# A hybrid S5 and attention decoder block: opening by single row tiles, modulation matmuls between product blocks, heads innermost in the bias table, gate row through DRAM

## Chip, cores and metric

The kernel runs on one core of a Trainium2 chip. The metric is the device time of one execution in microseconds, as the median of several runs. All times in the profile are microseconds from the start of the profiled execution's span.

## What is computed

One decoder block for 256 positions of width 2048, in float32. A conditioning vector c gives six modulation vectors (shift, scale and gate, for two sub-layers); the first sub-layer has an S5 and an attention branch side by side, the second is an MLP.

```
mod = silu(c) @ w_ada + b_ada                      # 2048 x 12288
sh1, sc1, g1, sh2, sc2, g2 = split(mod, 6)
h = rms_norm(x, g_mix) * (1 + sc1) + sh1
u, q, k, v, ga, gb = split(h @ w_in, ...)          # 2048 x 8192
y_ssm = s5_branch(u, ...)                          # complex scan, GELU, GLU
y_att = attention(q, k, v, rel_bias)               # 8 heads of 128, causal, T5 bias by distance
merged = sigmoid(ga) * (y_ssm @ w_proj_ssm) + sigmoid(gb) * (y_att @ w_proj_attn)
x = x + g1 * (merged @ w_out)
h2 = rms_norm(x, g_mlp) * (1 + sc2) + sh2
x = x + g2 * (square(relu(h2 @ w_ff1)) @ w_ff2)
out = rms_norm(x, g_final)
```

All 256 positions lie in one attention block, so attention is plain causal attention with a bias that depends on head and distance.

## The kernel before

**Products.** Every weight is read once from DRAM, in tiles of 128 rows by 1024 columns (512 KB). `stream` loads a tile into `wraw` (L132, L134; seven buffers), ScalarE casts it to a rounded high part `whi` and VectorE subtracts to get the low part `wlo` (`split`, L139 and L141; four buffers each). A product of activations and weights is then three matmuls: high by high, high by low and low by high (L171 to L173 in `gemm_t`, L209 to L211 in `gemm_n`, L185 and L187 in `gemm_d`). A tile of w_in costs 24 such matmuls in `gemm_t`, in eight column blocks `blk` of 128.

**Row tiles.** The 2048 columns of h are 16 row tiles `kt` of 128. h is kept transposed, as high and low part `ah` and `al`. Tile `kt` of h needs the matching 128 entries of scale and shift, `A1` and `B1`, and these need 128 columns of w_ada each.

**Order.** The instructions are written in program order, and a scheduler orders each engine's list at build time from priorities (`high_priority`) and explicit orders (`after`: not before that instruction on the same engine). At the end of each streamed tile `step` takes jobs out of *lanes*, each with its rate in jobs per tile. The lane `ada` carries the w_ada work, `ssm` the S5 tables, `second` what completes the opening, `xr` the scaling of x by the norm.

**Opening.** x (transposed) is loaded, `norm1` sums its squares with TensorE against a matrix of ones and makes the row R of reciprocal norms. For the first four row tiles, w_ada is multiplied on TensorE in `ada_first`: c stands as one column in a matrix of zeros (`cz`), four 32-column matmuls side by side (L240), a copy of the sums (L244), and a fold by a column of ones (L247). This is done in two halves of two row tiles, for scale and shift each, with 256 columns and four loads of 512 KB apiece. The first half precedes all products; the second (`second`) follows the second product tile. Then `scale1` (L369) multiplies x by R, and `make_h1` (L376 and `split`) makes h.

**The rest of w_ada.** For the other 12 row tiles `ada_job` loads rows of the transposed w_ada into the shared `wraw` buffers (L261), and VectorE multiplies with `cb`, the broadcast of silu(c), and sums along the row (L268): four loads of 512 KB for two row tiles' scale, four for their shift. `cb` comes by a one-partition row `crow`, a DRAM tile `cd`, and a broadcast load of 1 MB (L883). The lane runs at 1.65 jobs a tile until the ninth row tile's h is there, then at 0.8. The same kind of job later gives the two gates and the second modulation.

**Products of w_in.** The product units are walked as (columns, first and last row group), with row groups of 4, 6 and 6 row tiles: first q, k, v and u for row tiles 0 to 3, then the gate columns for 0 to 9 (its result is copied by L932), then four units over 4 to 9, and so on.

**Bias table.** `bias_prep` makes the bias by distance as 8 rows (one for each head) of 383, and one DMA on GpSimd's queue writes it 32 times into DRAM (`scr`, L397). `bias_load` reads it back skewed, so that partition p holds the bias of query p: `tz`, with head outermost (L404). `attn1` adds `tz` to the scores (L655, L656).

**Gate rows.** `ada_bcast` turns four columns of a modulation vector into a row on all partitions: four matmuls of a broadcast column against the identity (L288) and a copy by ScalarE (L290). It serves g1 and g2; g2's row `g2b` is first read when the MLP's next to last block of the second product ends.

Of the kernel before, what the change touches and what calls it, by code (L numbers as in the profile page):

```python
# [75 lines left out]
class Kern:  # L76
# [35 lines left out]

    def lane(self, name, jobs, rate, credit=0.0):
        self.lanes[name] = [list(jobs), rate, credit]
# [44 lines left out]
    def gemm_t(self, src, kts, c0, xh, xl, koff=0, mid=None):  # L159
# [3 lines left out]
        for i, (kt, hi, lo) in enumerate(self.stream(src, kts, c0)):  # L163
# [3 lines left out]
            for blk in range(8):  # L167
# [5 lines left out]
                self.mm = nc.tensor.matmul(o, lo[:, c], xh[:, kx, :], start=False, stop=sp, skip_group_check=True)  # L173
        return banks
# [42 lines left out]
    def ada_first(self, j, half, done, home=None):  # L217
        nc = self.nc
        n = 2 * (1 - j) + half
        st = {}  # L220

        def load(i):
            if home is None:
                w = st[i] = self.wp.tile([P, 1024], F32, name="wraw", tag="wraw", bufs=7)
            else:
                w = st[i] = home[:, i, :]
            with self.after(self.last):
                ld = nc.sync.dma_start(w, self.a["wan"][j, half, i])
            if self.early or home is not None:
                self.last = ld  # L230

        def total(i):
            w = st.pop(i).rearrange("p (k n) -> p k n", k=4)
            if i == 0:
                st["p"] = self.aux("adap")
            p = st["p"][:, 0:256]
            with self.after(None if self.early else self.mm):
                for k in range(4):
                    q = 32 * k
                    nc.tensor.matmul(p[q:q + 32, :], self.cz[:, 4 * i + k, :], w[:, k, :], start=i == 0,  # L240
                                     stop=i == 3, tile_position=(0, q), skip_group_check=True)
            if i == 3:
                acc = self.s4[:, 512 + 256 * n:768 + 256 * n]
                nc.scalar.copy(acc, p)  # L244
                pc = self.tmp("adac")
                for k in range(2):
                    self.adac = nc.tensor.matmul(pc[:, k:k + 1], acc[:, k * P:(k + 1) * P], self.ones[:, 0:1],  # L247
                                                 start=True, stop=True)
                done(pc[:, 0:2])
        return [(lambda i=i: load(i), lambda i=i: total(i)) for i in range(4)]  # L250

    def ada_job(self, vec, k0, n, done):
# [4 lines left out]
        def load(i):  # L257
            w = st[i] = self.wp.tile([P, 1024], F32, name="wraw", tag="wraw", bufs=7)
# [17 lines left out]
    def ahead(self, units):  # L276
# [5 lines left out]
        return [lambda i=i: job(i) for i in range(len(units) + 1)]  # L282

# [82 lines left out]
    def scale1(self, k0, gate=None):  # L366
        x = self.x[:, k0:k0 + 2, :]
        with self.after(gate):
            self.nc.vector.tensor_mul(x, x, self.R[:, None, :].to_broadcast([P, 2, S]))  # L369

    def make_h1(self, k0, A, B, fine=False):
        nc = self.nc
        h = self.big.tile([P, 2, S], F32, name="htmp", tag="htmp", bufs=1)
        for k, kt in enumerate((k0, k0 + 1)):
            with self.after(self.done[-1][1] if fine and k else None):
                nc.scalar.activation(h[:, k, :], self.x[:, kt, :], AF.Identity, scale=A[:, kt:kt + 1],  # L376
                                     bias=B[:, kt:kt + 1])
            if fine:
                self.split(self.ah[:, kt, :], self.al[:, kt, :], h[:, k, :])
        if not fine:  # L380
            self.split(self.ah[:, k0:k0 + 2, :], self.al[:, k0:k0 + 2, :], h)

    def bias_prep(self):
        nc, a = self.nc, self.a
        self.tt = self.slot("T", [P, 2, 1024], name="tt")
        oh, vec = self.tt[0:32, 0, 0:VL], self.tt[0:H, 1, 0:VL]
        rb = self.cp.tile([32, H], F32, name="rb", tag="rb")
        nc.gpsimd.dma_start(oh, a["onehot"])
        nc.gpsimd.dma_start(rb, a["rel_bias"])
        p = self.aux("bv")  # L390
        with self.after(self.mm):
            nc.tensor.matmul(p[0:H, 0:VL], rb, oh, start=True, stop=True)
        with self.after(self.done[-1][0]):
            nc.vector.tensor_copy(vec[:, 0:256], p[0:H, 0:256])
        nc.vector.memset(vec[:, 256:VL], NEG)
        self.scr = self.dr.tile([H, 32, VL], F32, name="scr")
        nc.gpsimd.dma_start(self.scr, vec[:, None, :].to_broadcast([H, 32, VL]))  # L397

    def bias_load(self):
        self.tz = self.slot("T", [P, H, S], name="tz")  # L400
        s = self.scr
        for g in range(4):
            src = bass.AP(tensor=s.tensor, offset=s.offset + 127 - 32 * g, ap=[[VL - 1, 32], [32 * VL, H], [1, S]])
            self.nc.gpsimd.dma_start(self.tz[32 * g:32 * g + 32], src)  # L404
# [106 lines left out]
    def ssm_cc(self):  # L511
        self.cc = self.slot("QT", [P, 2, 32, 4, 16], name="cc")
# [30 lines left out]
    def ssm_build1(self, part):  # L543
        c = self.cmp
        if part == 0:
            self.bp = self.slot("VT", [P, 2, 32, 4, 16], name="bp")
        bp = self.bp
# [68 lines left out]
    def ssm_builds(self):  # L616
        return ([self.bias_prep, self.ssm_load_bc] + [lambda: None] * 2 + [self.ssm_cc]
                + sum([self.parts(self.ssm_build1, i) for i in range(4)], [])
# [28 lines left out]
    def attn1(self, h):  # L647
# [7 lines left out]
        v.scalar_tensor_tensor(s[:, 0:128], p[:, 0:128], scale, self.tz[:, h, 128:256], op0=OP.mult, op1=OP.add)  # L655
        v.scalar_tensor_tensor(s[:, 128:384], p[:, 128:384], scale, self.tz[:, h, :], op0=OP.mult, op1=OP.add)  # L656
# [144 lines left out]
    def body(self):  # L801
        nc, a, v = self.nc, self.a, self.nc.vector
        with self.hot():
# [3 lines left out]
            crow = self.slot("S3", [P, D], name="crow")[0:1]  # L807
            nc.sync.dma_start(crow, a["c"])
# [472 lines left out]
```

## Time and profile before

| | us |
|---|---|
| median of 3 runs | 1431.3 (1429.15 to 1432.28) |
| profiled execution | 1430.27 |
| its span | 1428.5 |
| TensorE busy, whole span | 1376.4 |
| VectorE busy | 1055.6 |
| ScalarE busy | 706.0 |
| first product matmul starts | 27.39 |

The program moves 354.51 MB by DMA, a mean of 248 GB/s; nearly all are weight tiles on SP's queue. The busy time of TensorE counts matmuls from start to modelled end, so it holds waits shorter than a matmul's length. "PE" in the rows is TensorE, "PEld" its weight loads, "DVE" VectorE, "ACT" ScalarE, "POOL" GpSimd, "SP" the engine that issues most loads; "SPq" and "POOLq" are their DMA issues. In a timeline row the first two numbers are start and length, and the brackets at its end give the idle time before it and what ended that.

### The profile page before, as it was taken

The numbers are of one execution on the slowest core, as the hardware profiler recorded it, in microseconds if no ns is written. First come the engines' busy times: TensorE is split into PE (matmuls) and PEld (weight loads), VectorE is DVE, ScalarE is ACT, GpSimd is POOL, SyncE is SP. The second block draws the span as 40 slices with busy tenths as digits, with TensorE's granted clock in tenths as the row PEclk, the third lists the DMA queues.
The fourth block names the chain that finished last, engine by engine and source line by source line (L and its number), as shares of the span: only waits on it lengthen the run. The fifth ranks groups of instructions, "written<-read, shape, count | busy, mean of one in ns | idle before, by whom it ended". The sixth has DMA issues, their size and how long they took to land.

```text
span 1428.5 us, 23983 instructions
## 1 busy us (share of the span) xinstructions
PE 1376.4 (96%) x9562; PEld 1238.9 (87%) x9562; DVE 1055.6 (74%) x1509; ACT 706.0 (49%) x916; POOL 39.4 (3%) x90
## 2 busy tenths in 40 slices
PE   5889999999999999999899999999999999999996
PEld 4789999989989999988799988888888888888885
DVE  5887999876798788977686685778666555555676
ACT  4554444346645743445554555535363553635444
POOL 1000000400002100000000000000000000000000
PEclk9999999999999999999999999999999999999998
DMA  9999885786447998887598568778767566566551
GB/s 368 383 352 337 309 287 165 236 270 228 145 153 234 322 339 299 303 319 276 182 353 285 171 233 281 228 260 287 254 224 263 170 200 192 177 206 187 182 205 60
DMA packets 111491, 354.51 MB, mean 248 GB/s; under 512 B 12137, under 2 KB 12169, under 8 KB 111121
## 3 DMA queue, kind: packets, MB, share of 16 engines
q1 hardware_dynamic: 108482, 348.19, 71.3%
q0 software_dynamic: 2896, 4.79, 1.3%
q8 instruction: 75, 1.23, 0.3%
q14 instruction: 38, 0.31, 0.1%
HBM read 348.33 MB, written 2.50 MB: 246 GB/s over the span
## 4 chain that ended last, share of the span: by engine, by line
PE 82%; DVE 8%; DMA 6%; ACT 2%; issue 2%; DVEq 0%; SPq 0%; ACTq 0%
PE pd L185 12%; PE pn L209 11%; PE pn L210 11%; PE pn L211 11%; PE pt L171 9%; PE pt L173 9%; PE pt L172 9%; PE pd L187 6%; DMA wraw<-in_w_in_dram 4%; DVE wlo L141 2%; DVE wraw L268 2%; ACT whi L139 1%; DMA ahm<-in_wan_dram 1%; DMA wraw<-in_w_proj_attn_dram 1%; PE trv L564 1%
## 5 line engine op out<-in xcount | busy, mean ns | idle before, releaser
L139 ACT CAST whi<-wraw 128x1024 fp32r<-128x1024 f32 x456 | 476.1, 1052 | 597.7 <-PE pn L210 160.1
L141 DVE TENSOR_TENSOR wlo<-wraw,whi 128x1024 fp32r<-128x1024 f32 x456 | 553.6, 1223 | 278.4 <-ACT whi L139 276.3
L185 PE MATMUL pd<-h2h,whi 128*128 128x512 f32 x768 | 266.8, 395 | 0.4 <-DVE part L1156 0.4
L171 PE MATMUL pt<-ah,whi 128*128 128x256 f32 x896 | 251.4, 288 | 12.0 <-ACT ah L139 6.8
L172 PE MATMUL pt<-ah,whi 128*128 128x256 f32 x896 | 251.2, 286 | 0.0
L173 PE MATMUL pt<-ah,wlo 128*128 128x256 f32 x896 | 241.6, 288 | 5.2 <-DVE wlo L141 4.7
L268 DVE SCALAR_TENSOR_TENSOR wraw<-wraw,cb 128x1024 f32<-128x1024 f32 x176 | 213.9, 1220 | 0.0
L187 PE MATMUL pd<-h2h,wlo 128*128 128x256 f32 x768 | 209.0, 280 | 0.0
L210 PE MATMUL pn<-whi,ff 128*128 128x512 f32 x512 | 199.2, 389 | 0.0
L209 PE MATMUL pn<-whi,ff 128*128 128x512 f32 x512 | 198.5, 390 | 0.0
L171 PEld LDWEIGHTS pt<-ah,whi 128*128 128x128 f32 x896 | 172.2, 194 | 15.8 <-ACT ah L139 7.0
L211 PE MATMUL pn<-wlo,ff 128*128 128x512 f32 x512 | 182.9, 389 | 0.0
L173 PEld LDWEIGHTS pt<-ah,wlo 128*128 128x128 f32 x896 | 166.8, 194 | 8.5 <-DVE wlo L141 8.2
L172 PEld LDWEIGHTS pt<-ah,whi 128*128 128x128 f32 x896 | 173.5, 194 | 0.2
L185 PEld LDWEIGHTS pd<-h2h,whi 128*128 128x128 f32 x768 | 142.5, 188 | 32.0 <-issue 0.7
L187 PEld LDWEIGHTS pd<-h2h,wlo 128*128 128x128 f32 x768 | 144.8, 188 | 2.8
L209 PEld LDWEIGHTS pn<-whi,ff 128*128 128x128 f32 x512 | 96.1, 188 | 20.2 <-issue 0.2
L211 PEld LDWEIGHTS pn<-wlo,ff 128*128 128x128 f32 x512 | 96.1, 188 | 20.1
L210 PEld LDWEIGHTS pn<-whi,ff 128*128 128x128 f32 x512 | 96.1, 188 | 19.6
L171 PE MATMUL pt<-h2h,whi 128*128 128x256 f32 x256 | 72.4, 288 | 1.1 <-ACT h2h L139 1.1
L172 PE MATMUL pt<-h2h,whi 128*128 128x256 f32 x256 | 72.8, 286 | 0.0
L173 PE MATMUL pt<-h2h,wlo 128*128 128x256 f32 x256 | 71.8, 286 | 0.0
(338 smaller groups left out, 1762.4 us busy)
## 6 DMA issues: line engine op xcount, KB each, us to landing
wraw<-in_w_ff_dram SPq DMA_DIRECT2D x256, 512.0 KB, 4.9
wraw<-in_wat_dram SPq DMA_DIRECT2D x176, 512.0 KB, 5.8
wraw<-in_w_in_dram SPq DMA_DIRECT2D x128, 512.0 KB, 5.8
wraw<-in_w_out_dram SPq DMA_DIRECT2D x32, 512.0 KB, 6.8
wraw<-in_w_proj_attn_dram SPq DMA_DIRECT2D x16, 512.0 KB, 5.7
wraw<-in_w_proj_ssm_dram SPq DMA_DIRECT2D x16, 512.0 KB, 6.1
wraw<-in_wan_dram SPq DMA_DIRECT2D x8, 512.0 KB, 9.5
ahm<-in_wan_dram SPq DMA_DIRECT2D x8, 512.0 KB, 11.6
```

The costliest lines, as they stand in the source:

```text
L139: h = self.nc.scalar.copy(hi, src)
L141: s = self.nc.vector.tensor_sub(lo, src, hi.bitcast(F32))
L171: nc.tensor.matmul(o, hi[:, c], xh[:, kx, :], start=st, stop=False, skip_group_check=True)
L172: nc.tensor.matmul(o, hi[:, c], xl[:, kx, :], start=False, stop=False, skip_group_check=True)
L173: self.mm = nc.tensor.matmul(o, lo[:, c], xh[:, kx, :], start=False, stop=sp, skip_group_check=True)
L185: nc.tensor.matmul(banks[blk], hi[:, c], x2[:, :, kt, :], start=i + k == 0, stop=False, skip_group_check=True)
L187: self.mm = nc.tensor.matmul(banks[blk][:, S:2 * S], lo[:, c], x2[:, 0, kt, :], start=False, stop=i == n - 1 and k == 1, skip_group_check= ...
L209: nc.tensor.matmul(o, xh[:, kx, tk], hi[:, c], start=q == 0, stop=False)
L210: nc.tensor.matmul(o, xl[:, kx, tk], hi[:, c], start=False, stop=False)
L211: self.mm = last = nc.tensor.matmul(o, xh[:, kx, tk], lo[:, c], start=False, stop=q == n - 1)
L268: v.scalar_tensor_tensor(w, w, 1.0, self.cb[:, (i % 2) * 1024:(i % 2 + 1) * 1024], op0=OP.mult, op1=OP.mult, accum_out=pc[:, i:i + 1])
L564: nc.tensor.matmul(p[q, k * 64:(k + 1) * 64], self.VT[q, i, 8 * b + k, :], self.ident[q, q], start=True, stop=True)
```

## The change

It has these parts.

1. The opening goes by single row tiles: `ada_first` takes one row tile, with two loads of 512 KB and 128 columns for the scale and as many for the shift. Only row tile 0 precedes the products. Row tiles 1, 2 and 3 follow one product tile each (`follow`); the scale's matmuls are placed after the fourth column block of the product tile before (`self.mid`), the shift's after its last, and both folds after these.
2. After each of these three, eight matmuls whose result is never read (`idle`) follow the fold.
3. `cb` is made by TensorE (`ada_bcast`, four times) instead of through DRAM; `crow` and `cd` go.
4. The w_ada tiles for row tiles 4 to 15 go into slots that the opening has used (`ring`, `ringed`): eight at first, four for the last 24 loads. Each load is placed behind the multiplication that frees its slot. The S5 tables that use the same space come later (`drain`), and `ssm_cc` moves behind `ssm_build1`.
5. The bias by distance is made with positions on partitions, three columns of 128 by 8 heads. It is written to one DRAM row, copied 32 times DRAM to DRAM, and read with the heads innermost; `attn1` reads every eighth element.
6. g2's row goes as columns into a DRAM row in pieces of four bytes, and comes back in one broadcast load of 1 MB on GpSimd's queue.

```diff
+    def idle(self, n):
+        o = self.aux("unread")[:, 0:S]
+        for _ in range(n):
+            with self.after(self.adac):
+                self.nc.tensor.matmul(o, self.whi[:, 0:P], self.whi[:, 0:S], start=True, stop=True)
...
+                if blk == 3:
+                    self.mid = self.mm
+            self.whi = hi
...
-            with self.after(None if self.early else self.mm):
-                for k in range(4):
-                    q = 32 * k
-                    nc.tensor.matmul(p[q:q + 32, :], self.cz[:, 4 * i + k, :], w[:, k, :], start=i == 0,
-                                     stop=i == 3, tile_position=(0, q), skip_group_check=True)
...
+            with self.after(None if self.early else gate):
+                for k in range(8):
+                    q = 32 * (k % 4)
+                    m = nc.tensor.matmul(p[q:q + 32, :], self.cz[:, 8 * i + k, :], w[:, k, :], start=i == 0 and k < 4,
+                                     stop=i == 1 and k > 3, tile_position=(0, q), skip_group_check=True)
+            if i == 1:
+                acc = self.s4[:, 512 + P * n:640 + P * n]
+                self.acopy = nc.scalar.copy(acc, p)
+                st["acc"], st["last"] = acc, m
+
+        def fold(gate=None):
+            pc = self.tmp("adac")
+            with self.after(gate):
+                self.adac = nc.tensor.matmul(pc[:, 0:1], st["acc"], self.ones[:, 0:1], start=True, stop=True)
+            done(pc[:, 0:1])
...
-            w = st[i] = self.wp.tile([P, 1024], F32, name="wraw", tag="wraw", bufs=7)
+            w = st[i] = ring.pop(0) if ring else self.wp.tile([P, 1024], F32, name="wraw", tag="wraw", bufs=7)
...
+        def job(n, total):
+            total()
+            for i in free.get(n, ()):
+                loads[i]()
...
+        for c in range(2):
+            with self.after(self.mm):
+                nc.tensor.matmul(p[:, H * c:H * c + H], oh[:, c * P:(c + 1) * P], rb, start=True, stop=True)
...
-        self.scr = self.dr.tile([H, 32, VL], F32, name="scr")
-        nc.gpsimd.dma_start(self.scr, vec[:, None, :].to_broadcast([H, 32, VL]))
...
+        row = self.dr.tile([1, 3 * P * H], F32, name="scr1")
+        nc.gpsimd.dma_start(row[0].rearrange("(c p h) -> p c h", p=P, h=H), vec)
+        self.scr = self.dr.tile([32, 3 * P * H], F32, name="scr")
+        nc.gpsimd.dma_start(self.scr, row.to_broadcast([32, 3 * P * H]))
...
-            src = bass.AP(tensor=s.tensor, offset=s.offset + 127 - 32 * g, ap=[[VL - 1, 32], [32 * VL, H], [1, S]])
+            src = bass.AP(tensor=s.tensor, offset=s.offset + (P - 1 - 32 * g) * H,
+                          ap=[[3 * P * H - H, 32], [1, S * H]])
...
-        v.scalar_tensor_tensor(s[:, 0:128], p[:, 0:128], scale, self.tz[:, h, 128:256], op0=OP.mult, op1=OP.add)
+        v.scalar_tensor_tensor(s[:, 0:128], p[:, 0:128], scale, self.tz[:, 128:256, h], op0=OP.mult, op1=OP.add)
...
+            for i in range(4):
+                self.ada_bcast(rc[:, 4 * i:4 * i + 4], self.cb[:, i * 512:(i + 1) * 512])
...
+        def follow(kt):
+            def f():
+                with self.tc.high_priority(offset=OF1):
+                    parts = modn(kt, homes[kt], (self.mid, self.mm))
+                    for units, fold, last in parts:
+                        for ld, tot in units:
+                            ld()
+                    self.scale1(kt, n=1)
+                    totals(parts)
+                    self.idle(8)
+                    self.make_h1(kt, A1, B1, 1)
+                    self.gates = [(None, self.acopy)] + ([(None, self.done[-1][1])] * 3 if kt == 3 else [])
+            return f
...
+        ring = regs * 3 + regs[4:8] * 6
...
+        free = {None: range(8)}
+        free.update({i: (i + 8,) for i in range(16)})
+        free.update({i: (i + 4,) for i in range(20, 44)})
...
+        self.lane("second", [follow(kt) for kt in (1, 2, 3)], 1.0)
...
+        jobs = self.ringed(units, free)
+        self.lane("ada", [nop] * 3 + jobs[0:1] + [nop] * 2 + jobs[1:] + late, R1)
...
-            return lambda acc: self.ada_bcast(gcol(5, ch, acc), g2b[:, ch * 512:(ch + 1) * 512])
+            def f(acc):
+                row = g2d[0, ch * 512:(ch + 1) * 512]
+                nc.gpsimd.dma_start(row.rearrange("(k p) -> p k", p=P), gcol(5, ch, acc))
+                if ch == 3:
+                    nc.gpsimd.dma_start(g2b, g2d.to_broadcast([P, D]))
```

More of the change, by code (lines that the diff above doesn't have):

```diff
@@ L215, in gemm_n, with ada_first @@
         return banks
-    def ada_first(self, j, half, done, home=None):
+    def ada_first(self, j, kt, done, home=None, gate=None):
         nc = self.nc
-        n = 2 * (1 - j) + half
+        n = 4 * (1 - j) + kt
         st = {}
@@ L232, in total, with ada_job @@
         def total(i):
-            w = st.pop(i).rearrange("p (k n) -> p k n", k=4)
+            w = st.pop(i).rearrange("p (k n) -> p k n", k=8)
             if i == 0:
                 st["p"] = self.aux("adap")
-            p = st["p"][:, 0:256]
-            with self.after(None if self.early else self.mm):
-                for k in range(4):
-                    q = 32 * k
-                    nc.tensor.matmul(p[q:q + 32, :], self.cz[:, 4 * i + k, :], w[:, k, :], start=i == 0,
-                                     stop=i == 3, tile_position=(0, q), skip_group_check=True)
[L242 to L252, printed above, removed]
+            p = st["p"][:, 0:P]
+            with self.after(None if self.early else gate):
[12 more added lines that the diff above has]
+            done(pc[:, 0:1])
+        return ([(lambda i=i: load(i), lambda i=i: total(i)) for i in range(2)], fold, lambda: st["last"])
+    def ada_job(self, vec, k0, n, done, ring=None):
         nc, v = self.nc, self.nc.vector
@@ L364, in norm1, with scale1, make_h1 @@
         v.scalar_tensor_tensor(s, u, 1.5, s, op0=OP.add, op1=OP.mult)
-    def scale1(self, k0, gate=None):
-        x = self.x[:, k0:k0 + 2, :]
+    def scale1(self, k0, gate=None, n=2):
+        x = self.x[:, k0:k0 + n, :]
         with self.after(gate):
-            self.nc.vector.tensor_mul(x, x, self.R[:, None, :].to_broadcast([P, 2, S]))
-    def make_h1(self, k0, A, B, fine=False):
+            self.nc.vector.tensor_mul(x, x, self.R[:, None, :].to_broadcast([P, n, S]))
+    def make_h1(self, k0, A, B, n=2):
         nc = self.nc
         h = self.big.tile([P, 2, S], F32, name="htmp", tag="htmp", bufs=1)
[L374 to L381, printed above, removed]
+        for k in range(n):
+            kt = k0 + k
+            nc.scalar.activation(h[:, k, :], self.x[:, kt, :], AF.Identity, scale=A[:, kt:kt + 1],
+                                 bias=B[:, kt:kt + 1])
+        self.split(self.ah[:, k0:k0 + n, :], self.al[:, k0:k0 + n, :], h[:, 0:n, :])
     def bias_prep(self):
@@ L616, in ssm_builds @@
     def ssm_builds(self):
[L617 to L618 removed]
+        return ([self.bias_prep, self.ssm_load_bc] + [lambda: None] * 2
+                + sum([self.parts(self.ssm_build1, i) for i in range(4)], []) + [self.ssm_cc]
                 + sum([self.parts(self.ssm_build3, i) for i in (0, 1)], [])
```

111 lines of the change are left out of this document (64 added, 47 removed).

## The prediction

> **What bounds the kernel now.** I read the page first, then the windows by stage, then TensorE's timeline of the opening, then who waits for whom, and last the DMA view around each late weight tile.
>
> ```profile
> span 1428.5 us, 23983 instructions
> PE 1376.4 (96%) x9562; PEld 1238.9 (87%) x9562; DVE 1055.6 (74%) x1509; ACT 706.0 (49%) x916; POOL 39.4 (3%) x90
> 4.00:48.00 44.00, 30.38 (x256) 23.20 (x257) 28.70 (x117) 19.90 (x31) 1.46 (x4) 0.92 1.03 406
> 48.00:101.50 53.50, 47.41 (x320) 41.98 (x319) 48.49 (x83) 25.45 (x36) 0.00 (x0) 1.00 0.97 354
> 120.00:140.00 20.00, 18.62 (x140) 18.41 (x141) 16.69 (x23) 12.39 (x16) 0.00 (x0) 0.91 0.99 364
> 127.00:200.00 73.00, 73.00 (x545) 70.03 (x545) 70.66 (x103) 31.98 (x35) 0.00 (x0) 1.00 0.92 326
> 300.00:320.00 20.00, 17.82 (x133) 17.12 (x133) 15.37 (x28) 11.84 (x21) 0.00 (x0) 0.91 0.77 263
> 882.00:1107.00 225.00, 225.00 (x1127) 190.89 (x1126) 156.88 (x208) 112.78 (x133) 0.57 (x1) 1.00 0.75 250
> ```
>
> A window's row gives its length, the busy time of TensorE's matmuls and weight loads, VectorE, ScalarE and GpSimd, then the granted clock, the DMA share and the GB/s. TensorE has work 96% of the span; where a window is full (127 to 200, 882 to 1107) only fewer matmuls help. Time is lost ahead of that: in the opening, between 48 and 101.5, and at two places near 121 and 302 where the clock falls as well.
>
> ```profile
> 20.20 0.64 PE L240 MATMUL adap<-wraw,tz 128*32 128x256 f32 x8 [0.65 <-DMA wraw<-in_wan_dram]
> 21.33 0.61 PE L247 MATMUL adac<-s 128*128 128x1 f32 x4 [0.49 <-ACT s L244]
> 27.39 1.23 PE L171 MATMUL pt<-ah,whi 128*128 128x256 f32 x4 [5.46 <-ACT ah L139]
> 34.72 1.93 PE L240 MATMUL adap<-ahm,tz 128*32 128x256 f32 x32
> 37.68 1.93 PE L240 MATMUL adap<-ahm,tz 128*32 128x256 f32 x32
> 42.10 0.74 PE L171 MATMUL pt<-ah,whi 128*128 128x256 f32 x4 [1.39 <-ACT ah L139]
> 49.94 0.28 PE L172 MATMUL pt<-ah,whi 128*128 128x256 f32 x1
> 50.06 0.28 PE L173 MATMUL pt<-ah,wlo 128*128 128x256 f32 x1
> ```
>
> Product matmuls start 0.12 us apart at full clock (the last two rows). A row tile of w_in has 24 of them, so costs 2.9 us. The first product starts at 27.39. The second half's w_ada work then stops the products from 34.72 to 42.10, and the fourth tile ends near 42.1 + 48 x 0.12 = 47.9.
>
> ```profile
> 19.56 0.42 DVE L364 SCALAR_TENSOR_TENSOR R<-tz,R 128x256 f32<-128x256 f32 x1
> 20.23 1.29 DVE L369 TENSOR_TENSOR xt<-xt,R 128x512 f32<-128x512 f32 x2
> 24.99 1.21 DVE L141 TENSOR_TENSOR wlo<-wraw,whi 128x1024 fp32r<-128x1024 f32 x1
> 26.12 0.15 DVE L844 TENSOR_TENSOR B<-adac,cols 128x2 f32<-128x2 f32 x1
> 26.30 0.60 ACT L376 ACTIVATE htmp<-xt,B,A 128x256 f32<-128x256 f32 x1 [3.80 <-DVE B L844]
> cb<-cd SPq DMA_DIRECT2D x1, 1024.0 KB, 11.4
> ```
>
> The norm's row R is ready at 19.98. The shift's fold ended at 21.94, but its addition (L844) ran at 26.12, behind other VectorE work, and the first product waited for it.
>
> **Opening.** Four w_ada tiles instead of eight come first. The eighth arrived just before 20.20; tiles of 512 KB at the 406 GB/s of the first window take 1.3 us each, so the fourth lands near 15, before R. Then R decides: 19.98, one tile's scaling 0.42 (as wide as L364), and from L376's start at 26.30 to the product at 27.39 another 1.1, so near 21.5 with no delay in VectorE's queue. Broadcasting c by TensorE replaces the 1 MB of cb on the DMA queues (2.6 us at 406 GB/s). Its 16 broadcasts, at about 0.8 us for four (rows below), fill 3.2 us while TensorE waits for R, 15 to 21; without that cover they cost 3.2.
>
> Against this, three stops replace one. Per later row tile: 64 half-width w_ada instructions, and the gap from the last of them (37.68 + 1.93 = 39.61) to the product (42.10), 2.5 us. The instructions cost between 64 x 0.06 = 3.9 (no faster for half the columns) and half, 1.9; product matmuls go with width, 0.23 us for 512 columns (883.05 to 883.28, below) against 0.12 for 256, so I take 1.9. A tile then takes 2.9 + 1.9 + 2.5 = 7.3, and four end at 21.5 + 2.9 + 3 x 7.3 = 46.3: **1.6 us earlier**, from 6 earlier (gaps of 1.4 and R undelayed) to 10.3 later (first product still at 27.4, full-price instructions: 27.4 + 2.9 + 3 x 9.3 = 58.2). Eight unread matmuls, about 1 us, lie inside each gap and cost nothing unless ah comes sooner. The transfers allow this pace: five tiles per row tile, four of w_ada and one of w_in, are 6.6 us, so TensorE sets it by 0.7 us only; a faster cycle than 6.6 would wait for them.
>
> Removed beside that: the Silu over the one-partition row of c, its trip through GpSimd's queue to DRAM, and one small load ahead of x on SP. They were waited for by cb alone, so beyond the megabyte I count nothing.
>
> ```profile
> 121.34 0.39 PE L171 MATMUL pt<-ah,whi 128*128 128x256 f32 x1 [1.91 <-ACT whi L139]
> 122.00:126.00 4.00, 3.96 (x21) 3.75 (x20) 4.00 (x6) 2.27 (x5) 0.00 (x0) 0.59 1.01 379
> ACT whi L139 <- DMA wraw<-in_w_in_dram: 33.3, 18, 5.7
> scr<-tt POOLq DMA_DIRECT2D x1, 383.0 KB, 10.8
> wraw<-in_w_in_dram SPq DMA_DIRECT2D x128, 512.0 KB, 5.8
> 108.47 0.69 POOL L397 DMA_DIRECT2D scr<-tt  x1 [67.75 <-DVE tt L394]
> 110.34 9.80 DMA wraw<-in_w_in_dram
> 286.43 2.36 POOL L404 DMA_DIRECT2D tz<-scr  x4 [1.78 <-DMA u<-uT]
> 294.42 9.00 DMA wraw<-in_w_in_dram
> GB/s 410 419 391 419 401 419 428 410 364 401 410 410 410 401 410 410 419 419 392 370 357 329 171 94 97 89 78 106 114 256 293 127 187 228 228 264 309 319 300 228
> ```
>
> After 1.91 us without matmuls the granted clock fell to a mean 0.59 between 122 and 126. [...]
>
> **48 to 101.5, w_ada on VectorE.** These loads move from the shared seven buffers to slots of their own, eight deep, so w_in has all seven. ScalarE waited 33.3 us for w_in tiles between 20 and 130, and VectorE was idle 5.0 of these 53.5 us. That idle time is the most to be won while VectorE does the same multiplications and subtractions. I take half, **2.5**; the lane starts them one step later, up to 2.9 us, so the low end is nothing.
>
> The waits that come with it: a load into a used slot waits on SP until VectorE has multiplied what lay there, and behind it on SP stand the next w_in loads, for which ScalarE's cast and then TensorE wait. Today a load waits for one of seven shared buffers in the same way, so I count no loss, and the bound is the other 2.5 us of idle VectorE plus the step, 5 us, on either side. The first w_in casts wait for ScalarE's copy of w_ada sums; behind them stands L376, which needs the fold of that copy anyway. The S5 tables take the slots only when the lane has passed its eighth and, for cc, its last h.
>
> **Bias table.** The late w_in tiles, 9.80 and 9.00 us instead of the median 5.8, follow the two POOL transfers. The last row is the DMA view of 104 to 122 in 40 slices: after scr was issued the rate fell to some 90 GB/s. The new form writes the source from 128 partitions, repeats it in DRAM in 12 KB rows, and reads tz in 8 KB instead of 1 KB runs. Each stall is worth its idle time plus its clock loss: at 121, 20 - 18.62 + 20 x 0.09 = 3.2; at 302, 20 - 17.82 + 1.8 = 4.0. No row shows the new transfers; nothing to all is possible, and I take three quarters, **2.4 and 3.0**, because the queues they leave are still close to full. The added DRAM hop delays nothing: scr, issued at 108, is read at 286.
>
> ```profile
> L1089 DVE TENSOR_TENSOR ga<-ga,pt x8: 1081/1110/1118, 575.0 to 606.1; 128x512 f32<-128x512 f32 x8
> L1090 DVE TENSOR_TENSOR ga<-ga,gb x8: 684/693/705, 579.3 to 609.5; 128x512 f32<-128x512 f32 x8
> ```
>
> Its price is a strided read on VectorE. L1089 goes through SBUF four elements apart and takes 1110 ns, contiguous L1090 takes 693: 0.8 ns an element. Eight heads of 384 elements add 2.5 us of VectorE, beside 15.37 busy of 20 in 300 to 320, so I count nothing on the path; uncovered it would be 2.5. [...]
>
> **Gate row.**
>
> ```profile
> 881.93 1.05 PE L288 MATMUL adab<-ident,gc 128*128 128x128 f32 x8
> 882.74 0.48 PE L209 MATMUL pn<-whi,ff 128*128 128x512 f32 x1
> 883.05 0.39 PE L210 MATMUL pn<-whi,ff 128*128 128x512 f32 x1
> 883.28 0.39 PE L211 MATMUL pn<-wlo,ff 128*128 128x512 f32 x1
> L932 ACT COPY gp<-pt x4: 587/588/591, 123.8 to 126.9; 128x512 f32<-128x512 f32 x4
> 202.39 0.62 ACT L139 CAST ah<-htmp 128x512 fp32r<-128x512 f32 x1
> ```
>
> Four broadcasts hold TensorE for 882.74 - 881.93 = 0.81 us, four times over, where TensorE is full: **3.2 us** saved. The DRAM trip in its place uses GpSimd's queue (0.57 us busy in that window); the row is first read some hundreds of us after 1107. Its 4-byte pieces cost DMA time beside a 0.75 share; nothing waits. The bias product by two narrow matmuls instead of one of 383 columns saves at most 0.6; I take **0.4**.
>
> **Order.** The lane reaches its last w_ada tiles for h one step later. The last h was ready at 203.0. TensorE ends the first gate part, the 26th tile, near 126.9 (the last L932 copy), and reaches the last h 28 tiles later, 126.9 + 28 x 2.88 = 207.5; with one step less, about 1.6 us remains. I count nothing; the bound is 3 lost. The S5 builds move behind it with the same instructions, under full windows.
>
> **Sum.** 1.6 + 2.5 + 2.4 + 3.0 + 3.2 + 0.4 = 13.1. The span becomes 1415.4. The profiled execution took 1430.27, 1.8 over its span, and the median shown is 1431.3, 1.0 above it: 1418.2, **1418 us**.
>
> **Rivals.**
>
> Paced elsewhere (1424): VectorE and the DMA queues hold 48 to 101.5 to the old pace, so the earlier start runs into the same wait, and only half of the two stalls goes. Half of 3.2 + 4.0 is 3.6; with 3.2 + 0.4 that is 7.2, and 1431.3 - 7.2 = 1424. For it: VectorE 48.49 of 53.5, DMA share 0.97. Against: VectorE's 5.0 us of idle time there, and ScalarE's waits for w_in, which gets all seven buffers.
>
> Only TensorE's own saving (1429): the new DRAM transfers hit the same full queues, the stalls stay, and the extra gaps eat the start: 3.6 less up to 3 from the late last h, 1428 to 1431. This is also the case in which the change does not do what it says: the scheduler leaves L844's successor behind other VectorE work again, and the first product stays at 27.
>
> Three stops (1436, slower): place, 21 to 58 us. The price beyond the old opening is up to 10.3. It decides when the fourth tile ends after 47.9 + 3.6 + 2.9 = 54.4 and the stalls stay. With 10.3 lost, 3.6 saved and about 2 kept of the stalls, 1431.3 + 10.3 - 5.6 = 1436. For it: three gaps are certain. Against: R at 20 and four tiles' bytes by 15.
>
> **Chances.** Forecast 0.55, paced elsewhere 0.22, TensorE only 0.12, three stops 0.11. A measurement of this kernel can tell about 0.2%, 2.9 us, from no change. The first two are faster: 0.77; the third is the same: 0.12; the last slower: 0.11. The bounds put everything won at 6 + 5 + 3.2 + 4.0 + 3.2 + 0.6 = 22, 1409. The range runs from there to 1430, which leaves out the slower case and a little of the third.
>
> **What would show it.** First product near 21 and the fourth tile ending near 46; no 9 us w_in landing near 110 and 294, and granted clock 1.00 in both places; no L288 group after 850. I am wrong if the fourth tile ends after 50, if ScalarE still waits some 33 us for w_in before 130, or if a stop appears near 200.

## The result, and the profile after

| | before | after |
|---|---|---|
| median, us | 1430.8 (4 runs of the same chip) | 1422.3 (1421.3 to 1425.1, 4 runs) |
| ratio to before | 1 | 0.9944, interval 0.9929 to 0.9959 |
| profiled execution / its span | 1430.27 / 1428.5 | 1422.84 / 1421.0 |

The change is faster by 8.5 us, inside the range; the forecast 1418 had 4.3 us more. The total hides larger moves of both signs. Five landmarks that both traces have: the end of the fourth row tile's products, the last copy of the 26th tile's gate part (L932, now L982), its second half's first addition (`ga<-gp,pt`, now L980), the first of the last additions to v (now L956), and a point in the MLP near 830.

| stretch | before, us | after, us | difference | forecast |
|---|---|---|---|---|
| start to fourth tile's end | 47.9 | 50.8 | +2.9 | -1.6 |
| to the last copy of gp | 79.0 | 65.6 | -13.4 | -2.5 and -2.4 |
| to the first addition to ga | 104.5 | 112.0 | +7.5 | 0 |
| to the additions to v | 73.0 | 72.5 | -0.5 | -3.0 |
| to the MLP near 830 | 527.8 | 528.0 | +0.2 | 0 |
| to the end of the span | 596.4 | 592.2 | -4.2 | -3.2 |

The narrow bias matmuls (-0.4) can't be seen by themselves. These are TensorE's rows of the timeline after (start, length, idle time before and its releaser; "..." marks rows left out):

```profile
23.21 0.74 PE L177 MATMUL pt<-ah,whi 128*128 128x256 f32 x4 [3.56 <-ACT ah L145]
...
25.58 1.94 PE L249 MATMUL adap<-ahm,tz 128*32 128x128 f32 x32
...
28.97 1.08 PE L249 MATMUL adap<-ahm,tz 128*32 128x128 f32 x32
29.98 0.84 PE L259 MATMUL adac<-s 128*128 128x1 f32 x4
30.68 1.19 PE L117 MATMUL unread<-whi 128*128 128x256 f32 x8
32.31 0.73 PE L177 MATMUL pt<-ah,whi 128*128 128x256 f32 x4 [0.45 <-ACT ah L145]
...
40.11 0.74 PE L177 MATMUL pt<-ah,whi 128*128 128x256 f32 x4 [0.45 <-ACT ah L145]
...
47.89 0.74 PE L177 MATMUL pt<-ah,whi 128*128 128x256 f32 x4 [0.44 <-ACT ah L145]
...
196.85 0.39 PE L177 MATMUL pt<-ah,whi 128*128 128x256 f32 x1 [0.30 <-ACT whi L145]
198.11 0.39 PE L179 MATMUL pt<-ah,wlo 128*128 128x256 f32 x1 [0.76 <-DVE wlo L147]
202.06 1.22 PE L177 MATMUL pt<-ah,whi 128*128 128x256 f32 x4 [3.21 <-ACT ah L145]
...
299.74 0.38 PE L177 MATMUL pt<-ah,whi 128*128 128x256 f32 x1 [1.83 <-ACT whi L145]
301.00 0.58 PE L179 MATMUL pt<-ah,wlo 128*128 128x256 f32 x1 [0.76 <-DVE wlo L147]
```

The opening's cycle is 40.11 - 32.31 = 7.8 us a row tile, and the first, 9.1, holds a stretch at half clock behind the 3.56 us wait (granted clock 0.50 from 25.0 to 26.5; 32 narrow w_ada matmuls take 1.94 there and 1.08 later). Nothing stands at 121 any more. A new stop stands near 200, where TensorE waits 3.21 us for the last h, and the one at 300 has stayed. The windows after and, below them, before (length, busy TensorE, its weight loads, VectorE, ScalarE, GpSimd, granted clock, DMA share, GB/s):

```profile
48.00:116.00 68.00, 67.05 (x509) 64.44 (x510) 65.57 (x105) 38.52 (x53) 1.31 (x2) 1.00 0.98 381
116.00:185.00 69.00, 69.00 (x514) 66.17 (x513) 66.00 (x98) 28.69 (x33) 0.00 (x0) 1.00 0.92 325
185.00:215.00 30.00, 25.73 (x215) 24.51 (x214) 26.54 (x38) 10.47 (x14) 0.00 (x0) 0.94 0.54 185
290.00:310.00 20.00, 17.41 (x107) 15.97 (x106) 14.34 (x24) 6.90 (x8) 0.00 (x0) 0.91 0.89 290
```

```profile
48.00:116.00 68.00, 61.91 (x433) 55.54 (x432) 60.38 (x101) 33.23 (x45) 0.69 (x1) 1.00 0.97 355
185.00:215.00 30.00, 30.00 (x253) 30.00 (x251) 27.17 (x35) 14.15 (x15) 0.00 (x0) 1.00 0.80 271
```

From 48 to 116 TensorE now starts 509 matmuls where it started 433. From 185 to 215 it is the other way round, 215 against 253. ScalarE's 33.3 us of waits for w_in tiles between 20 and 130 are no longer in its list of waits.

Part of that early gain is borrowed. Of VectorE's 48 w_ada multiplications before the last h, these rows count those between the fourth tile's end and the gp copies (minimum, median and maximum in ns, first and last start), before and after:

```profile
L268 DVE SCALAR_TENSOR_TENSOR wraw<-wraw,cb x28: 1217/1220/1225, 46.8 to 124.8; 128x1024 f32<-128x1024 f32 x28
```

```profile
L279 DVE SCALAR_TENSOR_TENSOR ahm<-ahm,cb x25: 1217/1224/1233, 50.0 to 114.5; 128x1024 f32<-128x1024 f32 x25
```

With two earlier ones, 30 were done before, 25 after. Five of 1.22 us are 6.1 us of work put off, and the stretch behind gives back 7.5.

### The profile page after: what moved, and what is told of

The parts are those of the page before. It is cut to its first block, busy times and chain, and to the rows that moved or that the text cites. A ratio compares the mean times of both kernels' runs of the same rounds, so it can differ in the third digit from the quotient of the medians.

```text
span 1421.0 us, 24325 instructions
## 1 busy us (share of the span) xinstructions
PE 1376.6 (97%) x9716; PEld 1245.0 (88%) x9716; DVE 1057.4 (74%) x1517; ACT 700.4 (49%) x919; POOL 42.5 (3%) x95
## 4 chain that ended last, share of the span: by engine, by line
PE 87%; DVE 6%; DMA 3%; ACT 2%; issue 2%; SPq 0%; DVEq 0%; ACTq 0%
PE pd L194 12%; PE pn L218 11%; PE pn L219 11%; PE pn L220 11%; PE pt L177 11%; PE pt L178 10%; PE pt L179 10%; PE pd L196 6%; DVE wlo L147 2%; DMA wraw<-in_w_in_dram 2%; DVE wraw L279 1%; ACT whi L145 1%; PE trv L603 1%; DMA wraw<-in_w_proj_attn_dram 1%; PE rk L637 1%
## 5 line engine op out<-in xcount | busy, mean ns | idle before, releaser
L177 PE MATMUL pt<-ah,whi 128*128 128x256 f32 x896 | 252.2, 289 | 10.2 <-ACT ah L145 8.1
L179 PE MATMUL pt<-ah,wlo 128*128 128x256 f32 x896 | 246.7, 286 | 6.2 <-DVE wlo L147 6.2
L279 DVE SCALAR_TENSOR_TENSOR wraw<-wraw,cb 128x1024 f32<-128x1024 f32 x128 | 155.9, 1220 | 0.0
L177 PE MATMUL pt<-h2h,whi 128*128 128x256 f32 x256 | 72.5, 288 | 1.1 <-ACT h2h L145 1.1
```

Source lines behind the costliest of these rows:

```text
L177: nc.tensor.matmul(o, hi[:, c], xh[:, kx, :], start=st, stop=False, skip_group_check=True)
L279: v.scalar_tensor_tensor(w, w, 1.0, self.cb[:, (i % 2) * 1024:(i % 2 + 1) * 1024], op0=OP.mult, op1=OP.mult, accum_out=pc[:, i:i + 1])
```

## The experiments

Each was run beside the kernel before on the same chip; after is 1422.3 throughout. Four chips were used, on which the kernel before has medians of 1431.5 (first four runs), 1432.5 (next four), 1431.8 (next three) and 1432.3 us (last), against 1430.8 beside the changed kernel. So times of different groups compare to some 2 us only, and the ratios in brackets are the safer measure. The first question was what makes the last h late near 200.

**Lane's rate.** `-R2 = .8` / `+R2 = 1.0`

> The changed kernel with the w_ada lane at 1.0 instead of 0.8 jobs a tile after the ninth row tile. Theory A (order): the last h stands one step too late in the order, so the stop of 4.3 us idle time and 1.7 us of clock between 185 and 210 goes, and the time is 1416 to 1418. Theory B (VectorE is full): it is busy 66.0 of 69.0 us from 116 to 185, so the same work only comes earlier and TensorE waits for wlo instead; the stop shrinks, small waits before it grow, time 1420 to 1424.

Measured 1415.8 us (ratio 0.9889, 0.9874 to 0.9904). The time fell, but not where it should have: ScalarE made the last two parts of h (L410) at 202.7 and 203.2, where the changed kernel has them at 200.3 and 200.8, and TensorE waited 4.37 us for them. Up to the additions to v the run was 0.7 us behind the changed kernel; all the gain came later. Both theories missed: the rate in jobs per tile doesn't set the lane's pace.

**S5's builds after the last h.** The `ssm` lane stands still (`self.lanes["ssm"][1] = 0.0` in place of `SR1`) until the last h, then runs at `SR2 = 2.4` in place of 1.4.

> The changed kernel with the S5 table jobs stopped (rate 0 instead of 0.27) until the last h is made, and at 2.4 instead of 1.4 jobs a tile after that. Theory B: about 10 us of VectorE work leaves the full stretch, the last h is ready before TensorE needs it, no stop near 200, time 1415 to 1418. Theory A: the last h stands where it stood, the stop stays at 3 us or more, time 1420 to 1424.

Measured 1416.2 us (0.9892, 0.9874 to 0.9910). The last two parts of h still came at 201.9 and 202.4, with a wait of 4.36 us behind them, though VectorE was busy only 17.29 of the 23 us from 180 to 203. So VectorE's capacity isn't what holds the lane either.

**Old opening, all else changed.** `ada_first`, `second` and their loads by two halves, as before.

> The changed kernel with the opening by two halves of two row tiles as before (256 columns, one stop, no unread matmuls), everything else as changed: c broadcast by TensorE, slots of their own for w_ada, bias table, gate row. Theory C: three stops cost more than the earlier start gives, so the fourth tile ends at 46 to 48 instead of 50.8, the 26th at 111 to 114 instead of 117; the stop near 200 then eats most of it, time 1419 to 1423. Rival D: the single row tiles are what lets the w_ada lane run without waits; then 48 to 116 is slow again, the 26th tile ends after 119.

Measured 1415.1 us (0.9885, 0.9868 to 0.9902). The first product starts at 27.04, 3.8 later than in the changed kernel, yet its four row tiles end earlier: the first copy of the finished q block (`qk<-pt`) starts at 47.63, against 50.59 in the changed kernel and 46.42 before. Of these 3.0 us, 1.9 are left at the last gp copy (114.5 against 116.4), and the wait for the last h is 1.30 us in place of 3.21.

**No slots of its own.** `units += mod1(k0, 2, None)`, `jobs = self.ahead(units)`: the w_ada loads go back into the seven shared `wraw` buffers.

> The changed kernel with the w_ada loads for row tiles 4 to 15 in the seven buffers shared with w_in, one load ahead, as before. Theory E: the slots of their own made the 13 us gained between 48 and 127; then the 26th tile ends at 124 or later, ScalarE again waits over 20 us for w_in before 130, the stop near 200 is gone, and the time is 1423 to 1428. Rival F: the gain came from c being broadcast without the 1 MB load and from the new bias transfers; then the 26th tile ends by 119.

Measured 1428.7 us (0.9987, 0.9975 to 1.0). This is ScalarE's list of waits from 20 to 130 in this kernel, and one of its windows:

```profile
ACT whi L145 <- DMA wraw<-in_w_in_dram: 33.6, 19, 3.7
```

```profile
116.00:126.00 10.00, 10.00 (x86) 10.00 (x85) 9.71 (x17) 4.55 (x7) 0.52 (x1) 1.00 0.98 368
```

ScalarE's old waits for w_in are back, 33.6 us against 33.3, the last gp copy comes at 127.2 (116.4 in the changed kernel, 126.9 before), and the stop at 200 is gone. So the own slots bring most of the early gain, and with it the late debt; net they are worth 6.4 us. They aren't all of it. From the first copy of the finished q block (52.5) to the last gp copy this kernel takes 74.7 us, against 80.5 before and 65.8 in the changed one. And the window above is full, with the clock at 1.00: the stall at 121 is gone here too, though w_in has no more buffers than before. The new bias table is the nearest reason for that.

**No unread matmuls.** `self.idle(8)` left out.

> The changed kernel without the eight unread matmuls behind each of the three row tiles' w_ada groups; nothing else is different. Theory (a clock that stays up is worth something): the idle stretch of TensorE ahead of the first product of the second, third and fourth row tile grows from 0.45 us to some 1.6 us each, the granted clock falls behind at least some of them as it did behind the 3.56 us wait at 20 us, and a stretch of three microseconds then runs at 0.6 to 0.8: 0.7 to 1.5 us lost in each, 1424.4 to 1426.8 us against 1422.3. Rival (they only fill a wait that is there anyway, and waits of under 2 us keep the clock): the clock behind the gaps stays at 1.00, the fourth row tile ends at 50.8 us or up to 0.5 earlier, and the time is 1421 to 1423 us.

Measured 1420.7 us (0.9923, 0.9908 to 0.9939; the interval overlaps that of the changed kernel). Windows cut at the gaps:

```profile
32.00:40.50 8.50, 6.22 (x92) 5.27 (x92) 2.74 (x6) 3.03 (x7) 0.00 (x0) 1.00 1.03 408
40.50:49.80 9.30, 7.74 (x92) 6.42 (x92) 2.03 (x6) 2.40 (x6) 0.51 (x1) 0.82 1.03 408
```

TensorE now idles 1.50 us in each of the three gaps. Behind one of them the clock fell to a mean 0.82 and that cycle took 9.3 us in place of 7.8. So they do keep the clock up, as the theory had it, in one gap of three. But the gp copies come only 0.6 us (the first, 115.6) to 1.6 us (the last, 118.0) later, and at the end nothing of it is left: the clock is the theory's, the time the rival's.

**Old bias table.** `bias_prep`, `bias_load` and the two reads as before.

> The changed kernel with the bias table of the kernel before: heads outermost in the two scratch transfers and in tz, contiguous reads of tz; all else as changed. Theory of the prediction (the old table's transfers hold up the loads of w_in): the scratch transfer near 120 us is 1.5 MB again, TensorE waits for w_in beside it for 2 to 3 us, and the time is 1424.5 to 1426 us. Rival 1 (the lead that the own slots give covers that delay, and the table is worth nothing on the path): no wait for w_in near 120, 1421.5 to 1423 us. Rival 2 (the strided reads and the smaller pieces of tz cost more than they save): the wait at 300 us is 1 us or more shorter than the 2.6 us of the changed kernel, and the time is 1419 to 1421 us.

Measured 1419.9 us (0.9911, 0.9892 to 0.9931, which touches that of the changed kernel). The scratch transfer takes 10.2 us to land in place of 6.3, and the DMA rate from 116 to 126 falls to 278 GB/s, but TensorE is full:

```profile
116.00:126.00 10.00, 10.00 (x86) 10.00 (x85) 8.82 (x15) 5.01 (x6) 0.00 (x0) 1.00 0.83 278
```

In the total the new table is worth nothing that can be measured: rival 1, or better. Here the lead that w_in got from its seven buffers keeps the stall at 121 away by itself; the fourth run showed the stall gone without that lead. At 302 the waits (2.67 and 0.76) are no shorter, so rival 2's reason doesn't hold. The total hides two moves, though. At the first product of the S5 branch (`vr`) the run with the old table is 4.7 us behind (370.9 against 366.2). It has made that up by the gate `sg` (525.6 against 525.0), because TensorE waits 2.1 us in place of 6.4 between 310 and 530; more of these waits below.

**tz over all partitions.**

```diff
-            src = bass.AP(tensor=s.tensor, offset=s.offset + (P - 1 - 32 * g) * H,
-                          ap=[[3 * P * H - H, 32], [1, S * H]])
-            self.nc.gpsimd.dma_start(tz[32 * g:32 * g + 32], src)
+            src = bass.AP(tensor=s.tensor, offset=s.offset + (P - 1 - g) * H,
+                          ap=[[3 * P * H - 4 * H, 32], [1, S * H]])
+            self.nc.gpsimd.dma_start(tz[g::4], src)
```

> The changed kernel with the four transfers of the bias table into tz regrouped: each fills every fourth partition (32 partitions over the whole range) in place of 32 neighbours; the same values land in the same places. Theory (a transfer into 32 neighbouring partitions is what slows the other loads of the core): tz lands in well under the 10.0 us of the changed kernel, the DMA rate between 290 and 310 us stays over 300 GB/s, the waits for w_in at 299.7 and 301.0 us (1.83 and 0.76) shrink below 0.8 together, and the time is 1419.5 to 1421 us. Rival (it is the bytes and the queue's order, not where they go): tz takes 9 to 11 us, the waits stay at 2 to 3 us, and the time is 1421.5 to 1423 us.

Measured 1418.2 us (0.9905, 0.9887 to 0.9922), 4.1 below the changed kernel. The DMA view of the changed kernel, that of this one, and one window of this one:

```profile
tz<-scr POOLq DMA_DIRECT2D x4, 256.0 KB, 10.0
```

```profile
tz<-scr POOLq DMA_DIRECT2D x4, 256.0 KB, 6.3
```

```profile
290.00:310.00 20.00, 20.00 (x141) 18.78 (x140) 19.12 (x32) 10.42 (x17) 0.00 (x0) 1.00 0.89 324
```

The same bytes land in 6.3 us in place of 10.0, TensorE has no wait left there and its clock stays at 1.00. So it mattered where these bytes go; why neighbours are slower no run shows.

**Eight slots to the end.** On top of the kernel with S5's builds held back, which otherwise need these slots:

```
-ring = regs * 3 + regs[4:8] * 6
+ring = regs * 6
-free.update({i: (i + 8,) for i in range(16)})
-free.update({i: (i + 4,) for i in range(20, 44)})
+free.update({i: (i + 8,) for i in range(40)})
```

> The run with S5's builds held back until the last h, and the w_ada lane's own slots kept at eight to the end in place of four for the last 24 loads; nothing else differs from that run (1416.2 us, last h at 201.9 us, first product of the stop ending a wait of 4.36 us at 203.7). Theory (four slots cap the lane: a load is issued only behind its slot's multiplication and takes some 7 us to land): the last h comes before 198 us, the wait ahead of the products that read it is under 1.5 us, and the time is 1412 to 1415 us. Rival (the order of instructions fixed when the kernel is built paces the lane, one multiplication per tile step): the last h stays between 200 and 203 us, the wait is 3 to 4.5 us, and the time is 1415 to 1417 us.

Measured 1406.3 us (0.9821, 0.9806 to 0.9836): 9.9 below the same kernel with four slots (the second run), more than the theory asked. First that run, a view in each fence: VectorE's w_ada group between 116 and 185 (busy, mean ns), SP's waits between 116 and 215 (total, times, longest), the last six parts of h (first and last start), and VectorE's waits for casts between 150 and 204.

```profile
L279 DVE SCALAR_TENSOR_TENSOR ahm<-ahm,cb 128x1024 f32<-128x1024 f32 x19 | 22.8, 1217 | 0.0
```

```profile
SPq L272 <- DVE ahm L279: 16.1, 18, 2.5
```

```profile
L410 ACT ACTIVATE htmp<-xt,B,A x6: 584/592/609, 142.0 to 202.4; 128x256 f32<-128x256 f32 x6
```

```profile
DVE wlo L147 <- ACT whi L145: 6.1, 10, 1.7
```

The first three with eight slots, and the window of the stop:

```profile
L279 DVE SCALAR_TENSOR_TENSOR ahm<-ahm,cb 128x1024 f32<-128x1024 f32 x23 | 27.8, 1218 | 0.0
```

```profile
SPq L272 <- DVE ahm L279: 7.9, 11, 0.8
```

```profile
L410 ACT ACTIVATE htmp<-xt,B,A x6: 586/600/603, 127.8 to 188.9; 128x256 f32<-128x256 f32 x6
```

```profile
185.00:215.00 30.00, 30.00 (x253) 30.00 (x252) 25.68 (x32) 14.22 (x16) 0.00 (x0) 1.00 0.59 179
```

In the same 69 us VectorE multiplies 23 tiles in place of 19 (18 in the changed kernel). SP waits 7.9 us in place of 16.1 (22.9) for slots to come free, the last h comes 13.5 us earlier, and the stop is gone. So the number of slots makes the last h late.

It doesn't do so in the way that the theory had it. With four slots each of the last 24 loads is issued within 0.1 us of the end of the multiplication that frees its slot. But no multiplication waits for its tile: in the changed kernel and in the second run each of these 24 tiles has lain 4.5 to 11.3 us in its slot when VectorE comes to it. The last one of the changed kernel lands at 192.3 and is multiplied at 198.0. VectorE works down a list whose order is fixed when the kernel is built. In the second run that list takes splits and multiplications in turns ahead of the last h, and it is the splits that wait, for ScalarE's casts. So on the chip the order holds the lane, as the rival says, and eight slots changed that order. Why the scheduler places the multiplications so late with four slots no run shows.

**Old gate row.** `fin_g2` by `ada_bcast`, as before.

> The changed kernel with the gate row of the MLP made as before, by four groups of four matmuls and a ScalarE copy each; all else as changed. Theory (the sixteen matmuls lie on TensorE's path): the stretch from 828 us to the end is 3.2 to 4.5 us longer and the time is 1425.3 to 1427 us. Rival (what came off behind 828 us in the changed kernel is the order of the loads, not the matmuls): under 1 us more, 1421.5 to 1423.3 us.

Measured 1426.3 us (0.9967, 0.9953 to 0.9980): 4.0 more, 3.3 by the ratios. The stretch behind the MLP landmark is 3.9 longer. The gate row is worth what the theory said.

**The gains together.** Eight slots, and tz over all partitions.

> The run with the lane's own slots kept at eight to the end (1406.3 us), and the bias table's transfers into every fourth partition as in the run that did so alone (4.1 us less than the changed kernel). If the two gains come from different waits and add up: 1401.5 to 1403.5 us. If the earlier last h has already covered the wait at 300 us (0.69 us were left of it in the run with eight slots): 1405 to 1406.5 us.

Measured 1405.9 us (0.9828, 0.9804 to 0.9851). They don't add up: with eight slots only 0.69 us of the wait at 300 was left, although tz still took 9.9 us to land. The slow transfer cost only what the stream's lead didn't cover.

**The same with the old opening.**

> The same as the run with eight slots and spread transfers, with the opening of the kernel before, in two pairs of row tiles. Theory (the opening by single row tiles costs some 3 us at the fourth tile, and with the stop at 200 us gone nothing behind it takes that up): 2.5 to 4 us below the run with the new opening. Rival (the 7 us that the old opening brought in the changed kernel came from the stop at 200 us, by starting the lane earlier, and that stop is gone already): within 1 us of it.

Measured 1411.2 us (0.9859, 0.9834 to 0.9884), 5.3 more, so both missed. Its six runs spread from 1406.8 to 1413.8, and the interval overlaps that of the run before, so the size is uncertain. The four row tiles again end early, but the last gp copy comes 1.3 later than with the new opening, with a wait of 1.83 for an h at 110 and half clock behind it (matmuls start 0.21 us apart to 113.25, 0.12 after). This window of the old opening shows it:

```profile
106.00:116.00 10.00, 7.85 (x50) 7.24 (x49) 10.00 (x16) 4.64 (x7) 0.80 (x1) 0.83 1.03 406
```

By the first addition to ga it is 4.8 behind (223.2 against 218.4), with a second wait, 1.23 us at 153.6, for a split. The DMA queues were full (share 1.02 to 1.03) from 16 to 136 us in both. What makes that h and that split late was not traced further. So the opening's price, 3.0 us at the fourth tile, isn't its price at the end: that depends on what runs behind it.

**The same with the old bias table,** new opening, tz spread.

> The run with eight slots and spread transfers (1405.9 us), with the bias table of the kernel before (heads outermost, scratch of 8 source partitions, contiguous reads of tz) in transfers spread over every fourth partition in the same way. If the new table's layout is worth nothing on the path: 1404.9 to 1406.9 us. If its strided reads (2.7 us more of VectorE over all heads) lie on the path, which they may now that few waits are left: 1403 to 1404.9 us. If its shorter scratch transfer keeps a wait for w_in away near 120 us, where the DMA engines are full to 136 us in this kernel: a wait for w_in or its parts of over 1 us there, and 1407 to 1409 us.

Measured 1409.3 us (0.9834, 0.9820 to 0.9847), 3.4 more, nearest to the third case. It ran on another chip, and the intervals of the ratios overlap, so the total alone does not settle it. Two windows of it, and then the first of them in the kernel with the new table:

```profile
116.00:126.00 10.00, 10.00 (x86) 10.00 (x85) 8.88 (x17) 4.35 (x6) 0.00 (x0) 1.00 0.86 258
146.00:156.00 10.00, 8.73 (x56) 7.79 (x54) 10.00 (x14) 2.11 (x2) 0.00 (x0) 1.00 1.02 393
```

```profile
116.00:126.00 10.00, 10.00 (x84) 9.82 (x83) 10.00 (x17) 3.44 (x5) 0.32 (x1) 1.00 1.02 400
```

The rate slumps to 258 GB/s where the new table keeps 400, ScalarE waits 1.10 us for a tile of w_in at 139.9, and at 152.7 TensorE waits 1.27 us for a split. Of the 3.4 us, 0.9 lie ahead of the gp copies (114.4 and 115.4), where the table has no part; 1.7 come between there and ga (218.4 and 221.0). So the shorter scratch transfer may pay where the stream has no slack, by up to 1.7 of the forecast 2.4. That is argued, not shown: VectorE is busy 10.00 of the 10 us in which that split is late, and the run before, with the new table, has a like wait (1.23 us at 153.6).

## Why the prediction was right in sum, and where it was wrong

The direction and the order of size were right; two of the three marks that it named as "I am wrong" came true all the same (the fourth tile after 50, a stop near 200). Errors of both signs met, so that the total came within 4.3 us is in part luck. The rival "paced elsewhere" named 1424, which is nearer to 1422.3 than 1418. Its mechanism isn't what happened, though: it had the stretch from 48 to 101.5 at the old pace, and the stretch to the gp copies became 13.4 us shorter.

- **Opening, forecast -1.6, measured +2.9.** Half price for half the columns was right (32 in 1.0 us, where before 32 of twice the width took 1.93), and so was the pace: 7.8 a tile against 7.3. The gaps, counted as 2.5, are 29.98 to 32.31 = 2.3 from the fold on. What failed is "near 21.5 with no delay in VectorE's queue", which looks at VectorE alone. R ended at 18.65 and the scaled x at 20.42, but the addition L879 again stood behind the split of a weight tile, and L410 waited for it. VectorE's rows there, and ScalarE's:

```profile
20.69 1.23 DVE L147 TENSOR_TENSOR wlo<-wraw,whi 128x1024 fp32r<-128x1024 f32 x1
21.82 0.20 DVE L500 TENSOR_TENSOR tz<-tz 128x32 f32<-128x32 f32 x1
21.92 0.16 DVE L879 TENSOR_TENSOR B<-adac,cols 128x1 f32<-128x1 f32 x1
```

```profile
19.28 1.28 ACT L498 ACT_TABLE_LOAD   x1
20.83 0.56 ACT L324 COPY cb<-adab 128x512 f32<-128x512 f32 x1
22.12 0.60 ACT L410 ACTIVATE htmp<-xt,B,A 128x256 f32<-128x256 f32 x1 [0.72 <-DVE B L879]
```

  The first product came 1.7 late. L879 accounts for 0.7 of that, the wait of L410. Until 21.39 ScalarE was busy with work of its own: a table load for the S5 parameters' sine, and the last copy of the broadcast of c, whose matmuls the prediction counted as covered without asking for its copies. The half clock behind the long wait adds 1.3 in the first cycle (9.1 against 7.8), and three cycles 0.5 each.
- **48 to 101.5, forecast -2.5, at most 5.** The mechanism was right (w_in has all seven buffers, ScalarE's waits go), the size far off: -13.4 with the stall at 121 in it. The bound of 5 took VectorE's work in that stretch as fixed. It isn't: five multiplications moved out of it, and their time comes back in the next point.
- **The step that failed most: "so I count no loss"** for loads that wait on SP for their slot, and with it "Order", counted 0 with a bound of 3. Measured +7.5. Before, a load waits for any of seven buffers; here it waits for one given slot, and for the last 24 there are four. Rate (first run) and VectorE's capacity (second) were ruled out, and eight slots took the stop away, through the order of VectorE's list. "Order" had another fault, in its own terms. It set the last h against TensorE's arrival of before, 207.5, and found 1.6 us to spare, while the sum had TensorE 1.6 + 2.5 + 2.4 = 6.5 us earlier at the 26th tile, so there at 201.0. With the last h at 203.0 the stop was due unless the lane came forward as far. TensorE stood ready at 198.9, and the last h came at 202.0. Another 0.7 us of the wait is ScalarE's: it takes an S5 operation (`cc`, L552) ahead of L410, which starts at 200.3 where its B was ready at 199.6.
- **Bias table, forecast -2.4 and -3.0.** The stall at 302 was priced about right: it is worth 4.1 where it is removed by itself (forecast 4.0 for all of it). But the change leaves it standing, since tz takes 10.0 us in place of 8.7. The stall at 121 is gone with the new table and shared buffers (fourth run), and with the old table and own slots (sixth). Either is enough, so on top of the slots the table's 2.4 buy nothing that the total shows. "Reads tz in 8 KB instead of 1 KB runs" was the wrong cure: where the 32 rows go mattered more than how long they are (6.3 us into every fourth partition; into neighbours 10.0 in the long runs, 8.7 before and 10.4 in the sixth run in the short ones). The strided reads cost as estimated, 2.7 us over eight heads (397 + 644 ns each against 284 + 415); TensorE is full from 310 to 365, where most of them run.
- **Gate row, forecast -3.2.** Measured -4.2 in the trace, and 4.0 by undoing it (3.9 in that trace). Right.
- **Unread matmuls.** Counted at nothing, and nothing it is in the time, though without them the clock fell behind one gap of three (mean 0.82 from 40.5 to 49.8).

**Where three kernels gained.** The first, second and third run gained 6 to 7 us, though the stop at 200 grew in the first two and only shrank in the third. The main part lies between 365 and 500. This window is first of the changed kernel, then of the second run:

```profile
365.00:500.00 135.00, 128.56 (x1516) 126.35 (x1516) 121.33 (x165) 75.72 (x95) 15.34 (x32) 0.99 0.67 222
```

```profile
365.00:500.00 135.00, 135.00 (x1494) 133.47 (x1493) 122.99 (x168) 75.94 (x92) 15.39 (x32) 1.00 0.74 245
```

In the changed kernel TensorE stands still there for 6.4 us, in four waits: 2.42 at 377 and 1.34 at 426 for splits of weights that VectorE does behind steps of the S5 scan, 0.73 at 390 for a step of that scan, and 1.88 at 480 for a copy by ScalarE. The kernel before loses 6.1 in this window, so the change did not bring these waits. The first two runs have none of them, and the third loses 1.5. In the first two the waits at 300 are shorter or gone as well. The run with tz spread keeps 5.9 us of waits in this window, so its gain is the one at 300 alone.

**Open.** Why a faster lane, later S5 builds or the old opening take these waits away wasn't traced; VectorE's order differs there. With eight slots neither opening has any of them, which is part of why the old opening ends better with four slots and not with eight. The rest of that isn't settled.

## What to carry to other kernels

When loads get slots of their own, count the slots against the round trip: landing time plus the wait for the consumer. Then look which of the two waits: here the tiles lay ready, and the order of the consumer's list held them. When a forecast brings one engine forward, set every later meeting point against its new arrival. A lead won early can be work put off: count how many instructions of the late chain each stretch has done, before and after, before you book it. Spread the partitions of a narrow transfer before you lengthen its runs: here spreading took the landing from 10.0 us to 6.3, and the longer runs alone had left it at 10.0, where the short ones took 8.7 and 10.4.

## What the runs showed of the hardware that was not expected

- A transfer of 256 KB into 32 neighbouring partitions took 10.0 us to land, into every fourth partition 6.3 (7.6 and 6.6 in the tenth and eleventh run). With the old table's layout it was 10.4 into neighbours (sixth run) and 3.4 into every fourth (last run, which has eight slots besides).
- The clock fell behind short idle stretches. Behind 1.83 and 0.76 us at 300 the product matmuls started 0.21 us apart in place of 0.12 until 304.2 (granted clock 0.50 from 302 to 304.2). Without the unread matmuls TensorE idled 1.50 us in each of three gaps: behind one of them the clock had a mean of 0.82 (40.5 to 49.8), behind the others 1.00. What sets that one apart no run shows.
